# VectorE in place of accumulating DMAs for two chunks' down sums; S5 outputs one step later; the compression's small loads ahead

## The chip, the cores and the metric

One core of one Trainium2 chip runs the whole layer as one program. The metric is the device time in microseconds of one execution of that program. Its engines are TensorE (matmuls; PE in the profile, PEld for its weight loads), VectorE (DVE), ScalarE (ACT), GpSimd (POOL) and SyncE (SP, which here only issues DMAs).

## The reference, cut to what matters

One layer of a hybrid decoder on 256 tokens of width 2048, all in float32. The hidden width of both feed-forward halves is 5632.

```
def swiglu(x, w1, w3, w2):
    return (jax.nn.silu(x @ w1) * (x @ w3)) @ w2

h = h + 0.5 * swiglu(rmsnorm(h, ffn1_norm), ffn1_w1, ffn1_w3, ffn1_w2)
proj = rmsnorm(h, mix_norm) @ w_in
q, kc, vc, ksl, vsl, kw, vw, gates, u_ssm = jnp.split(proj, splits, axis=-1)
a = nsa_mixer(q, kc, vc, ksl, vsl, kw, vw, gates, ...)   # attention over compressed, selected and window keys
s = s5_mixer(u_ssm, ...)                                 # state space model, gelu, gated linear unit
h = h + jnp.concatenate([a, s], axis=-1) @ w_out
h = h + 0.5 * swiglu(rmsnorm(h, ffn2_norm), ffn2_w1, ffn2_w3, ffn2_w2)
out = rmsnorm(h, final_norm)
```

The attention compresses keys and values: each block of 32 positions plus a position table (`cmp_pe`) goes through a small two-layer network (`cmp_w1`, gelu, `cmp_w2`). The S5 mixer runs a scan over 64 complex states for each group of 16 channels, adds a skip term, and passes the result through gelu and a gated linear unit.

## The kernel before, in words

**Precision and weights.** A float32 product is made from three matmuls of halves: ScalarE makes the high half of a weight tile (`whi`), VectorE the low half (`wlo`), both in `split` (lines 138 and 139); TensorE multiplies high by high, high by low and low by high (lines 191 to 193). `wload` (line 163) has SyncE load 512 KB of weights, two tiles of 128 rows by 512 columns, into a buffer of the pool `raw`. `wtiles` feeds a loop of matmuls with such pairs.

**The feed-forward half-steps.** `ffn` goes through the hidden width in 11 chunks of 512. For a chunk it forms the gates (columns of `w1` and `w3`), then two of the four column blocks of the previous chunk's down product (`down(c - 1, prev, (0, 1))`), transposes the gates (line 435), and does the other two blocks (`down(c - 1, prev, (2, 3))`). The chunks of `wino` are special: there the gates of some tiles are formed with seven products in place of eight (`up_wino`). The first half-step has the special chunks 1 to 5, the second 1 to 10. `down` adds each 128 by 512 sum into the residual `h` in `add`: VectorE does so in one instruction (line 372), but for the special chunks ScalarE writes half the sum to a tile `d` of the pool `work` (line 369) and GpSimd issues a DMA that adds `d` into `h` (line 370).

**Pools and phases.** There are two layouts of the on-chip memory, `"ffn"` and `"mixer"`; `layout` closes the pools `w`, `work` and `raw` of one and opens those of the other in the same space (the mixer has 3 weight buffers of each half, 40 work and 5 raw buffers, and a pool of small tiles behind them). A tile of a new pool waits for the tiles of the old one that lay there. The pool `hidden` (8 buffers) stays through all phases. The first half-step changes to the mixer layout ahead of chunk 6, through `begin={6: go_on}`, and then runs the S5 preparation (`prepare`, line 691) beside the chunks 6 to 10; its first step loads seven small tensors into `work` (lines 476 to 484). The layout changes back ahead of the second half-step (line 1056).

**What sets the order.** The program is written in one order, and a planner of the framework fixes each engine's queue when the program is built: by priority (mostly the order of the program, with the weight splits 50 places ahead) among what it takes to be ready. Each engine then works through its queue in order. Side work is written as generators; `tick`, called after each weight tile pair, takes one step of each (`sides`), so their instructions stand between the matmuls.

**S5 and compression.** Two such generators run in the mixer. `s5_run` goes through eight tiles of 128 channels: `s5_tile` copies inputs to a padded tile (line 755), forms the input products (line 760), turns and scans the states (lines 763 to 772), turns them back into `xs5` (lines 774 to 780), and then forms the output with a group of small matmuls that read `xs5` (lines 783 and 787), the skip term (line 790), and for every second tile gelu and split into `hs`. `compress_all` starts when three of the four `hs` are there: `compress` loads the position table (line 817), transposes it (line 819), forms the blocks (line 828), loads `cmp_w1` and multiplies (lines 833 and 837), sums four partial results with a matmul (line 843) and applies gelu. Its second layer's weights are loaded on lines 855 and 856 and used on lines 858 and 867.

Of the kernel before, what the change touches and what calls it, by code (L numbers as in the profile page):

```python
# [72 lines left out]
def hymba_layer(tc, x, ffn1_norm, ffn1_w1, ffn1_w3, ffn1_w2, mix_norm, w_in,  # L73
# [4 lines left out]
    V, S, G, PE, SP = nc.vector, nc.scalar, nc.gpsimd, nc.tensor, nc.sync  # L78
    ctx = ExitStack()
    xp = ctx.enter_context(tc.tile_pool(name="xt", bufs=4))  # L80
    hp = ctx.enter_context(tc.tile_pool(name="hidden", bufs=8))
    cp = ctx.enter_context(tc.tile_pool(name="const", bufs=1))
    wp = sp = rp = mp = lay = None
    phase = ExitStack()
# [197 lines left out]
    def ffn(w1, w3, w2, xs, rstd, done, by_tokens=False, wino=range(0), begin={}):  # L282


        last = FF // 512 - 1

        def wpair(raw):
            hi, lo = (wp.tile([128, 2, 512], F32R, name=k, tag=k) for k in ("whi", "wlo"))
# [71 lines left out]
        def down(c, ht, ns):  # L360
            def hx(kt):
                a, b = ht[kt // 2 % 2]
                return a[:, kt % 2, :], b[:, kt % 2, :]

            def add(n, tt, p):
                o = h[:, tt, n * 512:(n + 1) * 512]
                if c in wino and c != last:
                    d = work([128, 512])
                    S.activation(d, p, AF.Copy, scale=0.5)  # L369
                    G.dma_start(o, d, accum_op=ALU.add)  # L370
                    return
                V.scalar_tensor_tensor(o, p, 0.5, o, op0=ALU.mult, op1=ALU.add)

            def tail(ns):

                for tt in range(NT):
                    t = slice(tt * 128, tt * 128 + 128)
                    for n in ns:
                        p = mm_tile()
                        for kt in range(4 * c, 4 * c + 4):  # L380
                            (xh, xl), (hi, lo) = hx(kt), ws[n, kt]
                            PE.matmul(p, xh[:, t], hi, start=kt == 4 * c, stop=False)
                            PE.matmul(p, xh[:, t], lo, start=False, stop=False)
                            PE.matmul(p, xl[:, t], hi, start=False, stop=kt == 4 * c + 3)
                        add(n, tt, p)
                        done(n, (tt,))

            ws = {}
            for n in ns:
                if by_tokens and c == last:  # L390
                    if n == 2:
                        tail((2, 3))
                    if n >= 2:
                        continue
                    for kb in (4 * c, 4 * c + 2):
                        raw = wload(w2[kb * 128:(kb + 2) * 128, n * 512 + 1024:n * 512 + 1536], 512)
                        hi, lo = wpair(raw)
                        for i in range(2):
                            ws[n + 2, kb + i] = hi[:, i, :], lo[:, i, :]
                for tt, p in enumerate(gemm_rows(hx, w2, n * 512, 512, 4 * c, 4 * c + 4)):  # L400
                    add(n, tt, p)
                if c == last:
                    done(n)
# [4 lines left out]
        for c in range(FF // 512 + 1):  # L408
            if c in begin:
                sides.append(begin[c]())  # L410
            if c == wino[0]:
                drain(comb)
            if c in wino:
                gates = up_wino(c)
            elif c < FF // 512:
                ps1 = gemm_rows(xs, w1, c * 512, 512)
                gates = []
                for tt in range(NT):
                    sl = work([128, 512])
                    S.activation(sl, ps1[tt], AF.Silu, scale=rstd[:, tt:tt + 1])  # L420
                    gates.append(sl)
                ps3 = gemm_rows(xs, w3, c * 512, 512)
                for tt in range(NT):
                    V.scalar_tensor_tensor(gates[tt], ps3[tt], rstd[:, tt:tt + 1], gates[tt],
                                           op0=ALU.mult, op1=ALU.mult)
            if prev is not None:
                down(c - 1, prev, (0, 1) if c < FF // 512 else (0, 1, 2, 3))
            if c < FF // 512:
                ht = []
                for kp in range(2):  # L430
                    ps = tp_tile().rearrange("p (k t) -> p k t", k=2)
                    for k in range(2):
                        for tt in range(NT):
                            f = (2 * kp + k) * 128
                            PE.transpose(ps[:, k, tt * 128:tt * 128 + 128], gates[tt][:, f:f + 128], ident)
                    hh, hl = (hp.tile([128, 2, T], F32R, name="hd", tag="hd") for _ in range(2))
                    split(hh, hl, ps)
                    ht.append((hh, hl))
                if prev is not None:
                    down(c - 1, prev, (2, 3))  # L440
                prev = ht
# [306 lines left out]
    def s5_tile(i):  # L748
# [29 lines left out]
        V.tensor_tensor(b, b, sn, ALU.mult)  # L778
        V.tensor_tensor(d, d, cs, ALU.mult)
        V.tensor_tensor(xs5[:, 1, :, 1:129], b, d, ALU.add)  # L780
        yield
        y = tp_tile()[:, :256].rearrange("p (r c) -> p r c", r=2)
        PE.matmul(y[:, 0, :], s5.k0[i // 4][:, i % 4, :], uv[:, 0, :], start=True, stop=False, skip_group_check=True)
        for r, m in ((0, s5.ca), (1, s5.c)):
# [12 lines left out]
            hs.append((hh, hl))  # L797

    def s5_run():
        for i in range(8):  # L800
            while len(ut) <= i // 2:
                yield
            yield from s5_tile(i)

    def gelu2(o, y, shape):

# [4 lines left out]
        V.scalar_tensor_tensor(o, t, 1.0, y, op0=ALU.add, op1=ALU.mult)  # L811


    def compress(kc, pe, w1, b1):

        pr = work([32, 128])
        SP.dma_start(pr, pe[0])
        ps = tp_tile()
        PE.transpose(ps[:, :32], pr, ident[:32, :32])
        pt = work([128, 32])  # L820
# [18 lines left out]
            yield  # L839
        hp = work([128, 128])  # L840
        V.tensor_copy(hp, hid)
        ps = tp_tile()
        PE.matmul(ps[:, :32], hp, cst[:, C_SEL:C_SEL + 32], start=True, stop=True)
        xh = work([128, 30])
# [2 lines left out]
        return xh  # L847

    def compress_all():
        while not kcv or len(hs) < 3:  # L850
            yield
        hk = yield from compress(kcv[0], cmp_pe_k, cmp_w1_k, par[:, P_B1:P_B1 + 1])
        hv = yield from compress(kcv[1], cmp_pe_v, cmp_w1_v, par[:, P_B1 + 1:P_B1 + 2])
        w2k, w2v = work([128, 128]), work([128, 128])
        SP.dma_start(w2k, cmp_w2_k[0])
        SP.dma_start(w2v, cmp_w2_v[0])
        ps = tp_tile()
        PE.matmul(ps[:, :30], w2k, hk, start=True, stop=True)
        G.memset(kcb, 0.0)
        V.tensor_scalar(kcb[:, :, 0:15], ps[:, :30].rearrange("p (g c) -> p g c", g=2), 0.5, None, ALU.mult)  # L860
        for g in range(2):
            yield
            hx = work([128, 8, 16])
            G.memset(hx, 0.0)
            V.tensor_scalar(hx[:, :, 0:15], hv[:, None, g * 15:g * 15 + 15].to_broadcast([128, 8, 15]), 0.5, None, ALU.mult)
            ps = tp_tile()
            PE.matmul(ps[:, :128], hx.rearrange("p a c -> p (a c)"), w2v, start=True, stop=True)
            m = [work([128, 4, 128]) for _ in range(2)]
            for b in range(8):
                V.tensor_scalar(m[b // 4][:, b % 4, :], ps[:, :128], cst[:, C_ROW + b:C_ROW + b + 1], None, ALU.mult)  # L870
            vcb.append(m)
# [258 lines left out]
```

## Time and profile before

| What | Value |
|---|---|
| Time, median of 3 runs | 1833.62 us (1832.59 to 1834.07) |
| The profiled execution | 1834.84 us, span of its instructions 1833.1 us |
| TensorE busy | 1788.7 us, 98% of the span |
| VectorE busy | 1518.7 us, 83% |
| ScalarE busy | 998.1 us, 54% |
| GpSimd busy | 112.8 us, 6% |
| Accumulating DMAs `h<-wk` | 112, 256 KB each, 5.9 us from issue to landing (median) |
| Mean granted clock of TensorE | 0.991 |

A busy share says how long an engine had an instruction in work, not what it waited for. The rows further down are therefore mostly of two kinds: timelines, in which a row gives the start, the duration, the line, the operation with output and inputs, and in brackets the idle time before it with what ended it; and waits, in which a row says which engine and line waited for which, with the total, the number of times and the longest. `x2` says that instructions of the same kind in a row are merged. Lines are those of the kernel before.

### The profile page before, as it was taken

How to read it: one execution, taken by the hardware profiler on the slowest of the kernel's cores; microseconds unless marked ns; L12 is line 12 of the kernel's file. 1: busy time of each engine (PE TensorE's matmuls, PEld its weight loads, DVE VectorE, ACT ScalarE, POOL GpSimd, SP SyncE). 2: the span in 40 equal slices, each digit the busy share in tenths (PEclk: the TensorE clock that was granted, in tenths of full speed). 3: DMA queues.
4: the chain of work that ended last, by engine and by line, in shares of the span. 5: the costliest groups of instructions: out<-in, count | busy, mean ns of one | idle time of the engine just before them, and what ended most of it. 6: DMA issues, size and time to landing. Idle time of an engine off the chain costs nothing.

```text
span 1833.1 us, 25026 instructions
## 1 busy us (share of the span) xinstructions
PE 1788.7 (98%) x9140; PEld 1489.4 (81%) x9140; DVE 1518.7 (83%) x2150; ACT 998.1 (54%) x1364; POOL 112.8 (6%) x145
## 2 busy tenths in 40 slices
PE   8999999969999999999999999999999999999997
PEld 6888888858888878899988777888888888888886
DVE  7999998846788887769887557999899998988994
ACT  7556656524433434544536745555666656666664
POOL 0001011100100000000000000000111011001103
PEclk9999999979999999999999999999999999999999
DMA  7557888676755666555574356556887788787884
GB/s 267 178 179 240 264 220 239 179 189 201 220 178 162 183 195 192 166 140 154 154 219 151 114 172 218 154 191 214 239 248 223 248 223 237 227 271 191 247 279 117
DMA packets 209424, 370.28 MB, mean 202 GB/s; under 512 B 22827, under 2 KB 32661, under 8 KB 209301
## 3 DMA queue, kind: packets, MB, share of 16 engines
q1 hardware_dynamic: 193172, 339.31, 58.3%
q0 software_dynamic: 16128, 29.37, 9.4%
q8 instruction: 72, 1.18, 0.3%
q14 instruction: 52, 0.42, 0.1%
HBM read 337.16 MB, written 2.11 MB: 185 GB/s over the span
## 4 chain that ended last, share of the span: by engine, by line
PE 50%; DVE 4%; issue 1%; ACT 0%; DMA 0%; ACTq 0%; SPq 0%; DVEq 0%
PE mm L193 7%; PE mm L192 7%; PE mm L191 7%; PE tp L303 3%; PE tp L305 3%; PE tp L306 3%; PE mm L306 2%; PE mm L303 2%; PE mm L305 2%; PE sd L306 2%; PE sd L305 2%; PE sd L303 2%; PE mm L203 1%; PE mm L202 1%; PE mm L204 1%; DVE wlo L139 1%
## 5 line engine op out<-in xcount | busy, mean ns | idle before, releaser
L138 ACT ACTIVATE whi<-raw 128x1024 fp32r<-128x1024 f32 x699 | 716.0, 1056 | 596.1 <-PE mm L193 225.9
L139 DVE SCALAR_TENSOR_TENSOR wlo<-raw,whi 128x1024 fp32r<-128x1024 f32 x699 | 835.8, 1222 | 211.1 <-ACT whi L138 210.0
L191 PE MATMUL mm<-whi,hd 128*128 128x512 f32 x688 | 270.0, 392 | 0.0
L192 PE MATMUL mm<-wlo,hd 128*128 128x512 f32 x688 | 268.3, 390 | 0.8 <-DVE wlo L139 0.8
L193 PE MATMUL mm<-whi,hd 128*128 128x512 f32 x688 | 268.3, 390 | 0.0
L191 PE MATMUL mm<-whi,xh 128*128 128x512 f32 x576 | 230.1, 401 | 18.0 <-ACT whi L138 18.0
L192 PE MATMUL mm<-wlo,xh 128*128 128x512 f32 x576 | 230.1, 399 | 1.6 <-DVE wlo L139 1.4
L193 PE MATMUL mm<-whi,xl 128*128 128x512 f32 x576 | 228.4, 397 | 0.0
L370 POOL DMA_DIRECT2D h<-wk x112 | 97.9, 972 | 1180.6 <-ACT wk L369 998.7
L192 PEld LDWEIGHTS mm<-wlo,hd 128*128 128x128 f32 x688 | 129.2, 188 | 27.5 <-DVE wlo L139 1.5
L191 PEld LDWEIGHTS mm<-whi,hd 128*128 128x128 f32 x688 | 129.2, 188 | 26.7 <-issue 0.6
L193 PEld LDWEIGHTS mm<-whi,hd 128*128 128x128 f32 x688 | 129.2, 188 | 26.7
L191 PEld LDWEIGHTS mm<-whi,xh 128*128 128x128 f32 x576 | 109.7, 191 | 42.1 <-ACT whi L138 19.6
L192 PEld LDWEIGHTS mm<-wlo,xh 128*128 128x128 f32 x576 | 110.1, 191 | 27.4 <-DVE wlo L139 5.0
L193 PEld LDWEIGHTS mm<-whi,xl 128*128 128x128 f32 x576 | 110.1, 191 | 22.5 <-DVE xl L139 0.4
L202 PE MATMUL mm<-xh,whi 128*128 128x256 f32 x384 | 111.8, 292 | 0.9 <-DVE wk L1008 0.9
L203 PE MATMUL mm<-xh,wlo 128*128 128x256 f32 x384 | 109.3, 285 | 1.1 <-DVE wlo L139 1.1
L204 PE MATMUL mm<-xl,whi 128*128 128x256 f32 x384 | 108.7, 283 | 0.0
L369 ACT ACTIVATE wk<-mm 128x512 f32<-128x512 f32 x112 | 65.6, 595 | 73.2 <-PE mm L193 69.7
L303 PE MATMUL sd<-whi,xh 128*128 128x512 f32 x255 | 99.2, 389 | 0.0
L303 PE MATMUL tp<-whi,xh 128*128 128x512 f32 x255 | 99.2, 389 | 0.0
L305 PE MATMUL tp<-wlo,xh 128*128 128x512 f32 x255 | 99.2, 389 | 0.0
(299 smaller groups left out, 2954.1 us busy)
## 6 DMA issues: line engine op xcount, KB each, us to landing
raw<-in_ffn_w_dram SPq DMA_DIRECT2D x528, 512.0 KB, 4.8
h<-wk POOLq DMA_DIRECT2D x112, 256.0 KB, 5.9
raw<-in_w_in_dram SPq DMA_DIRECT2D x48, 512.0 KB, 3.7
raw<-in_w_out_dram SPq DMA_DIRECT2D x32, 512.0 KB, 3.7
raw<-in_w_in_dram SPq DMA_DIRECT2D x8, 536.0 KB, 4.5
raw<-in_glu_w_dram SPq DMA_DIRECT2D x8, 512.0 KB, 3.7
h<-in_x_dram SPq DMA_DIRECT2D x4, 512.0 KB
raw<-in_cmp_w_k_dram SPq DMA_DIRECT2D x4, 512.0 KB, 4.2
```

The lines of the kernel that those rows point to most:

```text
L138: S.activation(hi, src, AF.Copy if isinstance(scale, float) else AF.Identity, scale=scale)
L139: V.scalar_tensor_tensor(lo, src, scale, hi.bitcast(F32), op0=ALU.mult, op1=ALU.subtract)
L191: PE.matmul(o, xh[:, t], hi[:, i, :n], start=kt == k0, stop=False)
L192: PE.matmul(o, xh[:, t], lo[:, i, :n], start=False, stop=False)
L193: PE.matmul(o, xl[:, t], hi[:, i, :n], start=False, stop=kt == k1 - 1)
L202: PE.matmul(o, wh, xh, start=kt == 0 and q % 2 == 0, stop=False, skip_group_check=True)
L203: PE.matmul(o, wl, xh, start=False, stop=False, skip_group_check=True)
L204: PE.matmul(o, wh, xl, start=False, stop=last, skip_group_check=True)
L303: PE.matmul(o, xh, wh, start=id(o) not in begun, stop=False)
L305: PE.matmul(o, xh, wl, start=False, stop=False)
L306: PE.matmul(o, xl, wh, start=False, stop=stop)
L370: G.dma_start(o, d, accum_op=ALU.add)
```

## The change

Three things are edited.

1. In `add`, the limit for the accumulating DMA is now `by_dma`. In the first half-step it is 4, so chunks 1 to 3 go by DMA as before and chunks 4 and 5 are added by VectorE like the ordinary chunks. In the second half-step it is 10, as before.
2. `s5_tile` ends with the states, and the output part is a generator of its own, `s5_out`. `s5_run` takes the first step of the next tile, then the output of the tile before it, then the rest of the tile.
3. `compress_all` loads the two position tables and the two second-layer weights at its first step, into four buffers of the pool `hidden` (renamed `hd`), rather than where they are used; and `compress` gives up its turn once more between the copy of the partial results and the matmul that sums them.

```diff
--- before.py
+++ after.py
@@ -78,7 +78,7 @@
     V, S, G, PE, SP = nc.vector, nc.scalar, nc.gpsimd, nc.tensor, nc.sync
     ctx = ExitStack()
     xp = ctx.enter_context(tc.tile_pool(name="xt", bufs=4))
-    hp = ctx.enter_context(tc.tile_pool(name="hidden", bufs=8))
+    hd = ctx.enter_context(tc.tile_pool(name="hidden", bufs=8))
     cp = ctx.enter_context(tc.tile_pool(name="const", bufs=1))
     wp = sp = rp = mp = lay = None
     phase = ExitStack()
@@ -283,6 +283,7 @@
 
 
         last = FF // 512 - 1
+        by_dma = last if last in wino else wino.stop - 2
 
         def wpair(raw):
             hi, lo = (wp.tile([128, 2, 512], F32R, name=k, tag=k) for k in ("whi", "wlo"))
@@ -364,7 +365,7 @@
 
             def add(n, tt, p):
                 o = h[:, tt, n * 512:(n + 1) * 512]
-                if c in wino and c != last:
+                if c in wino and c < by_dma:
                     d = work([128, 512])
                     S.activation(d, p, AF.Copy, scale=0.5)
                     G.dma_start(o, d, accum_op=ALU.add)
@@ -433,7 +434,7 @@
                         for tt in range(NT):
                             f = (2 * kp + k) * 128
                             PE.transpose(ps[:, k, tt * 128:tt * 128 + 128], gates[tt][:, f:f + 128], ident)
-                    hh, hl = (hp.tile([128, 2, T], F32R, name="hd", tag="hd") for _ in range(2))
+                    hh, hl = (hd.tile([128, 2, T], F32R, name="hd", tag="hd") for _ in range(2))
                     split(hh, hl, ps)
                     ht.append((hh, hl))
                 if prev is not None:
@@ -778,7 +779,10 @@
         V.tensor_tensor(b, b, sn, ALU.mult)
         V.tensor_tensor(d, d, cs, ALU.mult)
         V.tensor_tensor(xs5[:, 1, :, 1:129], b, d, ALU.add)
-        yield
+
+    def s5_out(i):
+
+        uv = ut[i // 2][:, i % 2, :].rearrange("p (c r) -> p r c", r=2)
         y = tp_tile()[:, :256].rearrange("p (r c) -> p r c", r=2)
         PE.matmul(y[:, 0, :], s5.k0[i // 4][:, i % 4, :], uv[:, 0, :], start=True, stop=False, skip_group_check=True)
         for r, m in ((0, s5.ca), (1, s5.c)):
@@ -797,10 +801,19 @@
             hs.append((hh, hl))
 
     def s5_run():
+        out = iter(())
         for i in range(8):
             while len(ut) <= i // 2:
-                yield
-            yield from s5_tile(i)
+                if next(out, out) is out:
+                    yield
+            tile = s5_tile(i)
+            next(tile)
+            yield from out
+            yield
+            yield from tile
+            out = s5_out(i)
+            yield
+        yield from out
 
     def gelu2(o, y, shape):
 
@@ -811,10 +824,8 @@
         V.scalar_tensor_tensor(o, t, 1.0, y, op0=ALU.add, op1=ALU.mult)
 
 
-    def compress(kc, pe, w1, b1):
-
-        pr = work([32, 128])
-        SP.dma_start(pr, pe[0])
+    def compress(kc, pr, w1, b1):
+
         ps = tp_tile()
         PE.transpose(ps[:, :32], pr, ident[:32, :32])
         pt = work([128, 32])
@@ -839,6 +850,7 @@
             yield
         hp = work([128, 128])
         V.tensor_copy(hp, hid)
+        yield
         ps = tp_tile()
         PE.matmul(ps[:, :32], hp, cst[:, C_SEL:C_SEL + 32], start=True, stop=True)
         xh = work([128, 30])
@@ -847,13 +859,13 @@
         return xh
 
     def compress_all():
+        pk, pv, w2k, w2v = (hd.tile([n, 128], F32, name="hd", tag="hd") for n in (32, 32, 128, 128))
+        for t, src in ((pk, cmp_pe_k), (pv, cmp_pe_v), (w2k, cmp_w2_k), (w2v, cmp_w2_v)):
+            SP.dma_start(t, src[0])
         while not kcv or len(hs) < 3:
             yield
-        hk = yield from compress(kcv[0], cmp_pe_k, cmp_w1_k, par[:, P_B1:P_B1 + 1])
-        hv = yield from compress(kcv[1], cmp_pe_v, cmp_w1_v, par[:, P_B1 + 1:P_B1 + 2])
-        w2k, w2v = work([128, 128]), work([128, 128])
-        SP.dma_start(w2k, cmp_w2_k[0])
-        SP.dma_start(w2v, cmp_w2_v[0])
+        hk = yield from compress(kcv[0], pk, cmp_w1_k, par[:, P_B1:P_B1 + 1])
+        hv = yield from compress(kcv[1], pv, cmp_w1_v, par[:, P_B1 + 1:P_B1 + 2])
         ps = tp_tile()
         PE.matmul(ps[:, :30], w2k, hk, start=True, stop=True)
         G.memset(kcb, 0.0)
```

## Rows read from the trace of the kernel before

**Rows 1.** The page, 40 equal slices: granted TensorE clock in tenths.

```profile
PEclk9999999979999999999999999999999999999999
```

**Rows 2.** Table of stretches: PE, PEld, DVE, ACT, POOL busy us (count), clock, DMA.

```profile
360.00:380.00 20.00, 15.31 (x72) 12.41 (x70) 1.29 (x2) 4.56 (x8) 6.93 (x14) 0.94 0.60 103
380.00:400.00 20.00, 9.76 (x21) 6.52 (x22) 11.25 (x45) 4.23 (x4) 0.18 (x2) 0.59 0.92 233
...
400.00:460.00 60.00, 60.00 (x270) 49.13 (x269) 42.41 (x103) 28.70 (x34) 4.35 (x6) 0.99 0.70 206
...
1125.00:1128.00 3.00, 3.00 (x8) 2.31 (x8) 3.00 (x5) 3.00 (x5) 0.00 (x0) 0.50 1.02 330
```

**Rows 3.** Timeline of TensorE, 374 to 402 us: start us, us, line, idle before.

```profile
374.69 0.39 PE L192 MATMUL mm<-wlo,hd 128*128 128x512 f32 x1
374.92 0.39 PE L193 MATMUL mm<-whi,hd 128*128 128x512 f32 x1
385.88 1.22 PE L191 MATMUL mm<-whi,xh 128*128 128x512 f32 x2 [10.57 <-ACT whi L138]
387.14 0.80 PE L192 MATMUL mm<-wlo,xh 128*128 128x512 f32 x1
...
395.82 1.22 PE L191 MATMUL mm<-whi,xh 128*128 128x512 f32 x2 [4.27 <-ACT whi L138]
...
401.45 0.40 PE L191 MATMUL mm<-whi,xh 128*128 128x512 f32 x1
```

**Rows 4.** Timeline of ScalarE, 384 to 396 us.

```profile
384.78 1.06 ACT L138 ACTIVATE whi<-raw 128x1024 fp32r<-128x1024 f32 x1 [8.83 <-DMA raw<-in_ffn_w_dram]
...
394.71 1.06 ACT L138 ACTIVATE whi<-raw 128x1024 fp32r<-128x1024 f32 x1 [8.88 <-DMA raw<-in_ffn_w_dram]
```

**Rows 5.** Waits of SyncE's queue, 350 to 400 us: total, times, longest.

```profile
SPq L163 <- DMA h<-wk: 37.2, 1, 37.2
```

**Rows 6.** Timeline of SyncE's queue, 375 to 396 us.

```profile
380.91 0.37 SPq L163 DMA_DIRECT2D raw<-in_ffn_w_dram  x1
381.33 0.46 SPq L476 DMA_DIRECT2D wk<-in_ssm_lam_re_dram  x1
...
389.08 3.46 SPq L163 DMA_DIRECT2D raw<-in_ffn_w_dram  x5
```

**Rows 7.** Instructions on tile h, VectorE's line: durations min, median, max.

```profile
L372 DVE SCALAR_TENSOR_TENSOR h<-mm,h x64: 679/685/774, 106.1 to 1823.2; 128x512 f32<-128x512 f32 x64
```

**Rows 8.** Timeline of TensorE, 362.5 to 366 us: the transposes of the gates.

```profile
363.35 1.04 PE L435 MATMUL tp<-cst,wk 128*128 128x128 f32 x8
```

**Rows 9.** Timeline of GpSimd, 358 to 362 us.

```profile
359.53 0.74 POOL L722 MEMSET ones<- 128x128 f32 x1
```

**Rows 10.** Timeline of VectorE, 1113 to 1120 us, second layout change.

```profile
1113.67 1.23 DVE L139 SCALAR_TENSOR_TENSOR wlo<-raw,whi 128x1024 fp32r<-128x1024 f32 x1 [2.57 <-ACT whi L138]
```

**Rows 11.** Timeline of SyncE's queue, 1112 to 1120 us.

```profile
1114.92 3.52 SPq L163 DMA_DIRECT2D raw<-in_ffn_w_dram  x7
```

**Rows 12.** Timeline of TensorE, 1119 to 1130 us, second layout change.

```profile
1123.51 0.73 PE L191 MATMUL mm<-whi,xh 128*128 128x512 f32 x2 [1.18 <-ACT whi L138]
...
1124.79 0.65 PE L192 MATMUL mm<-wlo,xh 128*128 128x512 f32 x1 [0.56 <-DVE wlo L139]
...
1128.54 0.39 PE L193 MATMUL mm<-whi,xl 128*128 128x512 f32 x1
```

**Rows 13.** Waits of TensorE, 790 to 975 us: total, times, longest.

```profile
PE tp L787 <- DVE xs L780: 1.3, 2, 0.7
...
PE tp L819 <- DMA wk<-in_cmp_pe_v_dram: 0.6, 1, 0.6
PE tp L787 <- DVE xs L776: 0.5, 1, 0.5
PE sd L760 <- ACT upad L755: 0.4, 1, 0.4
```

**Rows 14.** Line 755, the copies ahead of the input matmuls.

```profile
L755 ACT ACTIVATE upad<-wk x64: 297/316/336, 792.2 to 922.3; 32x128 f32<-32x128 f32 x64
```

## The prediction

> **What bounds the kernel now.** I read the slices of the page first: the only one in which TensorE's granted clock falls to 7 tenths is the ninth, 367 to 412 us [rows 1]. The table by stretches shows what that is: from 360 to 380 us TensorE is busy 15.31 of 20 us, from 380 to 400 us 9.76 of 20 at a mean clock of 0.59, and VectorE does 1.29 us of work in the first of the two [rows 2]. Elsewhere TensorE streams, as the stretch from 400 to 460 us does (60.00 of 60). So the place to look at is this hole, and not VectorE, busy as it is.
>
> TensorE's timeline gives its size. The last matmul of chunk 4's second down half starts at 374.92; the first of chunk 6 at 385.88 after 10.57 us of idling, a second hole of 4.27 us ends at 395.82, and full rate is back at 401.45 [rows 3]. Between 374.92 and 401.45 there are 24 matmuls, the 12 of each of two weight tiles. At the 0.23 us between starts before the hole (374.69 to 374.92) 25 steps take 5.75 us; they took 26.53. **The hole costs 20.8 us.**
>
> What ends it? TensorE waits for ScalarE's split of the raw weights (384.78, 394.71), and that for the load [rows 4]. SyncE's own waits say why the load is late: 37.2 us for one thing, the DMA that adds chunk 4's down sums into `h` [rows 5]. Its timeline: the first load of the new phase at 380.91, then seven small loads for the S5 preparation (381.33 onward), the second weight load only at 389.08 [rows 6]. So the chain is: last matmul, ScalarE's halving copy, GpSimd's issue, DMA landing shortly before 380.9, all of it because the copies `d` lie in the work pool of the old layout, over which the new pools are laid; then SyncE's issue, 4 us of load, the split. The second hole is the seven small loads' 7.75 us (381.33 to 389.08) on SyncE's queue ahead of load two.
>
> **The change, part by part.**
>
> *Down sums of chunks 4 and 5 on VectorE.* It removes 16 ScalarE copies, 16 GpSimd issues and 16 DMAs and adds 16 VectorE operations of 0.685 us, 11.0 us in all [rows 7]. Chunk 4's eight run between 358 and 377 us, where VectorE is nearly idle [rows 2]: nothing. Chunk 5's eight (5.5 us) follow from about 440 us on, in a stretch where VectorE has 17.6 of 60 us free [rows 2], but also TensorE's low halves to make on time; I take 0 and keep 5.5 for the range. If that cover were gone, TensorE would wait on `wlo`, as it does in later, fuller stretches.
>
> What matters is that nothing of chunk 4 is left in the old work pool after the transposes of chunk 5's gates, which end at 364.4 (363.35 plus 1.04) [rows 8]. Then the new raw pool should open some 16 us earlier. Two rows say that pools open one by one and not with the whole layout: the memsets in the mixer's small pool ran at 359.53, while chunk 4's down sums were still being multiplied [rows 9], and at the change back to the FFN layout SyncE issued seven raw loads in a row from 1114.92, the moment VectorE's last split of the old raw pool was done (1113.67 plus 1.23), while TensorE still worked [rows 10, 11]. So loads one to five (five raw buffers) go out near 364.4 and are there by 370. They also pass the seven small loads in SyncE's queue: these need the new work pool, over the old weight tiles, which TensorE reads to 375.3, and the planner orders by readiness (the memsets passed GpSimd work that the program has before them).
>
> **What is late next** is the new weight pool: it lies over the old weight tiles, so the first split waits for the last matmul's end, 374.92 plus 0.39 = 375.31. From the split's start to the first matmul is 1.10 us, and 2.36 us to the first that needs the low half (384.78 to 385.88 and 387.14) [rows 3, 4]. So it starts at 375.4, the third matmul at 377.76 instead of 375.61: 2.15 us remain. Then the clock: 380 to 400 us has a mean granted clock of 0.59 [rows 2]. At the second layout change the gaps are only 1.18 and 0.56 us, and still 1125 to 1128 us was granted 0.50, which is 1.2 GHz [rows 2]; 1124.79 to 1128.54 is 10 steps in 3.75 us instead of 2.3 [rows 12]. That is the nearest case, and I take its 1.5 us (0 to 1.7). The hole shrinks from 20.8 to 3.7 us (2.15 + 1.5): **17.1 us gained**, bounds 5.5 (rivals below) and 20.8 (no wait for the weight pool at all).
>
> The Trainium skill (TensorE: Matmul & The Clock Gate, Part 1) holds that only an idle gap of some length brings the clock down, and shorter ones leave it; by it the 1.5 us would not be paid and the total would be 1813.0. The rows of the second layout change speak against that, since gaps of 1.18 and 0.56 us are followed by half clock there.
>
> The seven small loads then occupy SyncE from 375.4 to 383.2, and load six can be split 5.6 us later (389.08 to 394.71 for the nearest one), at 388.8; TensorE has it at 389.9. Five tiles of 12 matmuls at 0.23 us last TensorE to 377.3 (two steps before 377.76) + 13.8 + 1.5 = 392.6. It fits with 2.7 us to spare, so the second hole goes too.
>
> *S5 outputs one step later.* The group of 17 small matmuls of an output now stands behind the next tile's first two input matmuls, and VectorE's skip-add behind two multiplications (2 x 0.68). No instruction is added, and a pair of tiles still takes eleven steps. TensorE's waits for the states are 1.3 and 0.5 us in 790 to 975 us [rows 13]; they should mostly go.
>
> *Small loads of the compression ahead, two steps more.* The loads move from the middle of the stage to SyncE's queue at its start, past weight loads that wait for free raw buffers there: four issues of about 0.5 us, hidden. TensorE's wait of 0.6 us for the position table goes [rows 13]. The two added steps delay attention by two ticks, which the GLU and output products cover. Parts two and three have 2.4 us of waits to win; reordering can also make new ones, at worst the longest of these, 0.7 us, at each of the eight outputs, 5.6 us. The old waits name their cause and the new ones would need one, so I take **2.0 us**, with 2.4 and minus 5.6 as ends.
>
> **Sum.** The profiled execution took 1834.84 us (span 1833.1 and 1.7 around it); 1834.8 - 17.1 - 2.0 = 1815.7. The median of the runs shown is 1833.62, 1.2 less, so the forecast is **1814.5 us**. The likeliest case's own range is 1810 to 1820.
>
> **Rivals.**
>
> (a) *The small loads keep their place ahead of load two.* Then load one is early, but SyncE stands at the first small load until 375.3 and load two goes out at 383.2 instead of 389.08. Only that 5.9 us is won: 1833.6 - 5.9 - 2.0 = 1825.7. For it: this is their order now [rows 6]. Against: now all become ready at one moment, and then they will not.
>
> (b) *The raw pool waits for the last matmul too.* Load one at 375.4 instead of 380.91 is 5.5 us: 1826. Against: the second layout change, where raw loads went out with TensorE still reading weights.
>
> (c) *The change does not open the pool*: another tile holds it as long. The hole stays and only the 2.0 us come: 1831.6, not told from no change. Against: SyncE's only long wait names the DMA [rows 5].
>
> (d) *Slower: TensorE meets the next tile's input before ScalarE has it.* Those input matmuls now stand ahead of the outputs, in order, and need eight ScalarE copies of 0.316 us (2.5 us) [rows 14], with a 1.06 us weight split possibly before them: 3.6 us on seven tiles, 25 us, so 1833.6 - 17.1 + 25 = 1841.5. It decides from 2.5 us per tile (7 x 2.5 = 17.5 against 17.1). Against: the same copies stood before the same matmuls so far and cost TensorE 0.4 us [rows 13].
>
> **How the numbers follow.** Forecast 0.74, (a) 0.09, (b) 0.07, (c) 0.05, (d) 0.05. A measurement of this kernel tells 0.2%, 3.7 us, from no change. Faster: forecast, (a) and (b), 0.90; within it: (c), 0.05; slower: (d), 0.05. The range goes from 1810 (20.8 and 2.4 us both won give 1810.4) to 1828, which takes in (a) and (b) with a part of the 5.5 us of VectorE or of the 5.6 us of new waits lost.
>
> **What would show it.** In the trace after: no wait of SyncE for the accumulating DMA near 375 us; five raw loads near 364, ahead of the seven small ones; TensorE's gap at the layout change under 2 us and no second one; chunk 6 some 17 us earlier against the transposes of chunk 5; no TensorE wait for the position table, little for the states. The prediction is wrong if raw loads still start after 375 us, if the small loads come before load two, if chunk 5's sums make `wlo` late, or if the stage from 780 to 975 us grows.

## The result, and the profile after

The changed kernel takes **1815.62 us** (median of 4 runs, 1813.4 to 1817.65), the kernel before on the same chip 1833.69 us (4 runs, 1832.59 to 1834.07). The ratio is 0.9902, with a 95% interval of 0.9885 to 0.9919: 18.1 us, or 1.0%, faster. The forecast was 1814.5 us, the range 1810 to 1828. The profiled execution took 1816.18 us, with a span of 1814.4 us and a mean granted clock of 0.996.

Line numbers have moved: 372 is 373 in the changed kernel, 435 is 436, 477 stands for 476, 727 is 728, 755 is 756, 787 is 791, and the compression's sums, 837 before, are line 848.

The page of the changed kernel: busy time by engine, the clock in 40 slices, and the accumulating DMAs that are left (96, where there were 112).

```profile
PE 1783.4 (98%) x9140; PEld 1488.5 (82%) x9140; DVE 1528.2 (84%) x2166; ACT 990.0 (55%) x1348; POOL 99.0 (5%) x129
...
PEclk9999999999999999999999999999999999999999
...
L371 POOL DMA_DIRECT2D h<-wk x96 | 84.0, 977 | 1044.3 <-ACT wk L370 862.8
```

The slice at 7 tenths [rows 1] is gone. The table of stretches of the changed kernel (busy us of PE, PEld, DVE, ACT, POOL with counts, then clock, DMA share, GB/s) answers to [rows 2]:

```profile
360.00:380.00 20.00, 18.33 (x85) 14.61 (x84) 9.90 (x13) 4.08 (x6) 1.83 (x9) 1.00 0.53 148
380.00:400.00 20.00, 20.00 (x90) 16.58 (x89) 17.36 (x60) 8.57 (x10) 0.00 (x0) 1.00 0.94 263
400.00:460.00 60.00, 58.79 (x267) 48.26 (x266) 47.61 (x125) 24.79 (x27) 0.78 (x3) 1.00 0.63 188
```

From 360 to 460 us TensorE idles 1.67 + 0 + 1.21 = 2.9 us, where it idled 14.9, and the clock stays full. Between the transposes of chunk 5's gates and those of chunk 6's it now takes 433.82 - 363.03 = 70.8 us; before it was 451.61 - 363.35 = 88.3. So **17.5 us of the 18 come from the layout change alone**. Timeline of TensorE, the start in chunk 6 before (chunk 5's is in [rows 8]), then both starts in the changed kernel:

```profile
451.61 1.03 PE L435 MATMUL tp<-cst,wk 128*128 128x128 f32 x8
```

```profile
363.03 1.03 PE L436 MATMUL tp<-cst,wk 128*128 128x128 f32 x8
...
433.82 1.03 PE L436 MATMUL tp<-cst,wk 128*128 128x128 f32 x8
```

Timeline of SyncE's queue in the changed kernel, 342 to 401 us (a row gives start and duration of a merged run of issues), which answers to [rows 6]:

```profile
342.27 24.31 SPq L163 DMA_DIRECT2D raw<-in_ffn_w_dram  x7
374.99 0.34 SPq L477 DMA_DIRECT2D wk<-in_ssm_lam_re_dram  x1
...
381.62 0.58 SPq L485 DMA_DIRECT2D wk<-in_ssm_c_im_dram  x1
382.30 18.03 SPq L163 DMA_DIRECT2D raw<-in_ffn_w_dram  x10
```

The merged first row holds the last two loads of the old layout (342.27 and 343.40) and five of the new one, the first at 364.10; it ends at 342.27 + 24.31 = 366.58. These five are the ones that used to go out at 380.91 and from 389.08 on. The seven small loads stand behind them, from 374.99. SyncE's waits from 340 to 400 us (total, times, longest) show the same: no DMA into `h` is among them any more [rows 5].

```profile
SPq L163 <- DVE wlo L139: 13.4, 5, 10.5
SPq L477 <- PE mm L193: 8.4, 1, 8.4
...
SPq L163 <- PE tp L436: 3.3, 1, 3.3
```

The second row is the small loads' wait for the last matmul on the old weight tiles, the third the new raw loads' wait for chunk 5's transposes. VectorE's timeline shows what took the place of the eight DMAs of chunk 4, the first of four such pairs up to 374.32 us:

```profile
357.11 1.37 DVE L373 SCALAR_TENSOR_TENSOR h<-mm,h 128x512 f32<-128x512 f32 x2 [0.48 <-PE mm L193]
```

TensorE's timeline over the change, which answers to [rows 3]:

```profile
374.57 0.39 PE L193 MATMUL mm<-whi,hd 128*128 128x512 f32 x1
376.11 0.73 PE L191 MATMUL mm<-whi,xh 128*128 128x512 f32 x2 [1.15 <-ACT whi L138]
377.37 0.50 PE L192 MATMUL mm<-wlo,xh 128*128 128x512 f32 x1 [0.53 <-DVE wlo L139]
377.70 0.40 PE L193 MATMUL mm<-whi,xl 128*128 128x512 f32 x1
...
405.39 0.24 PE L535 MATMUL tp<-cst,wk 32*128 32x32 f32 x1 [1.21 <-DVE wk L528]
```

Two gaps of 1.15 and 0.53 us are left of 10.57 and 4.27, full rate follows at once, and there is one new wait: the small transposes of the S5 preparation (line 535) for VectorE, 1.21 us.

Later, in the mixer's stage, something got worse. TensorE's waits from 780 to 975 us in the changed kernel, against [rows 13]:

```profile
PE sd L848 <- DMA raw<-in_cmp_w_v_dram: 2.6, 1, 2.6
...
PE tp L791 <- DVE xs L777: 0.5, 1, 0.5
...
PE tp L791 <- DVE xs L781: 0.2, 1, 0.2
```

The waits for the states fell from 1.8 to 0.7 us and the one for the position table is gone, but the value sums of the compression now wait 2.6 us for their own weights, which is more than the 1.7 us that these two gave.

### The profile page after: what moved, and what is told of

It is laid out like the page before. It is cut to its first block, busy times and chain, and to the rows that moved or that the text cites. A ratio compares the mean times of both kernels' runs of the same rounds, so it can differ in the third digit from the quotient of the medians.

```text
span 1814.4 us, 24981 instructions
## 1 busy us (share of the span) xinstructions
PE 1783.4 (98%) x9140; PEld 1488.5 (82%) x9140; DVE 1528.2 (84%) x2166; ACT 990.0 (55%) x1348; POOL 99.0 (5%) x129
## 3 DMA queue, kind: packets, MB, share of 16 engines
q8 instruction: 72, 1.18, 0.3%
## 4 chain that ended last, share of the span: by engine, by line
PE 52%; DVE 3%; issue 1%; DMA 1%; ACT 0%; ACTq 0%; DVEq 0%
PE mm L193 7%; PE mm L192 7%; PE mm L191 7%; PE tp L304 3%; PE tp L306 3%; PE tp L307 3%; PE mm L307 3%; PE mm L304 3%; PE mm L306 3%; PE sd L307 2%; PE sd L304 2%; PE sd L306 2%; PE mm L202 2%; PE mm L203 2%; PE mm L204 2%; DVE wlo L139 1%
## 5 line engine op out<-in xcount | busy, mean ns | idle before, releaser
L371 POOL DMA_DIRECT2D h<-wk x96 | 84.0, 977 | 1044.3 <-ACT wk L370 862.8
L307 PE MATMUL sd<-whi,xl 128*128 128x512 f32 x255 | 99.2, 389 | 0.0
```

The source lines that it names most:

```text
L307: PE.matmul(o, xl, wh, start=False, stop=stop)
```

## The experiments

Theory: the gain is the early opening of the raw pool at the first layout change, by the down sums alone, and the queue order that comes with it; parts two and three together give nothing, because one of their pieces makes the new wait. The rivals: parts two and three have a share of the gain; both chunks' sums are needed; early loads alone do it, whatever SyncE issues next.

### One part alone: e1 and e2

e1, against the kernel before:

```
+        by_dma = last if last in wino else wino.stop - 2
...
-                if c in wino and c != last:
+                if c in wino and c < by_dma:
```

> Only part one: VectorE adds the down sums of chunks 4 and 5; S5 and compression as before. Theory: this part carries the whole gain, 17 to 18 us by TensorE's timeline up to chunk 6 (the transposes of chunk 6's gates come 17.5 us earlier in the changed kernel), so about 1816.2 us. Rival: the VectorE additions cost some 2 us later on and parts two and three win them back: then about 1818.

e2, against the changed kernel:

```
-                if c in wino and c < by_dma:
+                if c in wino and c != last:
```

> Only parts two and three: S5 outputs a step later, small loads ahead, the added steps; chunks 4 and 5 by accumulating DMA as before. Theory: no measurable change, 1833.7 within 1 us, because the 2.4 us of waits that go are replaced by TensorE's new wait of 2.6 us for the last load of the compression's value weights and slower matmuls behind it; the 20.8 us hole at the layout change is unchanged. Rival, as predicted: 2.0 us faster, about 1831.7.

Measured: e1 1816.91 us (ratio 0.9909, 0.9893 to 0.9924). e2 1833.35 us (0.9997, 0.9988 to 1.0005): no change. The longest of TensorE's waits in e2 are the old hole and the new wait for the value weights:

```profile
PE mm L191 <- ACT whi L138: 18.5, 4, 10.5
...
PE sd L848 <- DMA raw<-in_cmp_w_v_dram: 2.2, 1, 2.2
```

So the down sums carry the whole gain, and the other two parts give nothing when taken together: the forecast's 2.0 us for them is refuted as a net figure.

### One of the two chunks: e5

Chunk 4's sums by VectorE, chunk 5's still by DMA (the other parts undone):

```
-                if c in wino and c != last:
+                if c in wino and (c < by_dma or by_dma < c < last):
```

> Part one for chunk 4 alone: VectorE adds its down sums, chunk 5 goes by accumulating DMA as before; S5 and compression as before. Theory: only the copies that lie in the old work pool at the layout change matter, and chunk 5's already lie in the new one, so the hole is closed as with both chunks: 1816 to 1817 us, TensorE's waits at the change 1.1 and 0.5 us. Rival: chunk 5's DMAs cost something of their own in the following 80 us: 1818 or more.

Measured: 1816.26 us (0.9901, 0.9886 to 0.9916), and the waits from 360 to 460 us are those of the changed kernel:

```profile
PE mm L191 <- ACT whi L138: 1.1, 1, 1.1
PE tp L535 <- DVE wk L528: 1.0, 1, 1.0
PE mm L192 <- DVE wlo L139: 0.5, 1, 0.5
```

Chunk 4's eight copies alone held the pool. Chunk 5's eight additions are neither needed nor a burden: with them (e1) and without them the time is the same within the runs. One thing differs from the changed kernel: half clock follows the two gaps in e5's trace, some 1.5 us (last section).

### The queue order: e8

The changed kernel, with the four weight loads after the first held behind the last of the seven small loads:

```
+        follow = behind and len(held) < 4
+        with tc.issue_after(behind[0]) if follow else nullcontext():
+            SP.dma_start(raw[:, :kq, :n], src.rearrange("(k p) n -> p k n", p=128))
...
-        SP.dma_start(cn[1], c_im[0].rearrange("(i g) h p -> (g h) i p", g=8))
+        behind.append(SP.dma_start(cn[1], c_im[0].rearrange("(i g) h p -> (g h) i p", g=8)).ins)
```

> The changed kernel with the next four weight loads after the first one of the mixer layout held behind the seven small loads in SyncE's queue, as they stood before. Theory: the order in that queue is worth the second hole: SyncE stands at the first small load to 375.0, load two goes out near 382.3, can be split 5.6 us later at 387.9, and TensorE, done with tile one at 380, has it at 389.0; 9 us of hole and 1.7 us of slow matmuls, about 1826 us. Rival: the small loads' DMAs take little and load two lands in 4 us with a shorter queue: 3 to 5 us slower than the changed kernel, about 1820.

Measured: 1824.79 us (0.9949, 0.9934 to 0.9963), 9.2 us over the changed kernel. SyncE's queue, and TensorE's longest wait:

```profile
364.11 0.37 SPq L165 DMA_DIRECT2D raw<-in_ffn_w_dram  x1
375.01 0.34 SPq L482 DMA_DIRECT2D wk<-in_ssm_lam_re_dram  x1
...
382.11 9.60 SPq L165 DMA_DIRECT2D raw<-in_ffn_w_dram  x6
```

```profile
PE mm L196 <- ACT whi L138: 14.5, 4, 10.2
```

This is rival (a), built as an experiment: it gives half of the gain back. It was priced at 1825.7, 0.9 us off. That the planner put five weight loads ahead of the small ones is worth 9 us by the medians, and the prediction gave this rival the highest chance of the four (0.09). At the layout change itself the price is higher: from chunk 5's transposes to chunk 6's e8 takes 445.01 - 363.05 = 82.0 us, 11.2 more than the changed kernel. Part of that comes back in the mixer's stage, where its wait for the value weights is 1.6 us and not 2.6 and the clock stays full behind it.

### Where parts two and three lost their gain: e3, e4, e7, e11

e3 undoes part three (the small loads of the compression, and its added step); e4 undoes part two; e7 takes only the added step out (one line, which runs once for the keys and once for the values, so it is the prediction's two added steps); e11 keeps it and gives the last eight blocks of value weights a place of their own.

```
e3     def compress(kc, pe, w1, b1):
+        pr = work([32, 128])
+        SP.dma_start(pr, pe[0])
...
e7         V.tensor_copy(hp, hid)
-        yield
         ps = tp_tile()
...
e11 +        early = [hd.tile([128, 512], F32, name="hd", tag="hd") for _ in range(2)]
+        for q, t in enumerate(early):
+            SP.dma_start(t.rearrange("p (l n) -> p l n", n=128),
+                         cmp_w1_v[0][(24 + 4 * q) * 128:(28 + 4 * q) * 128, :].rearrange("(l p) n -> p l n", p=128))
```

> Parts one and two, the compression as before (its small loads where they are used, no added step). Theory: TensorE's wait of 2.6 us for the value weights is gone, the wait of 0.6 us for the position table is back, the waits for the states stay low: about 1814, 1 to 2 us faster than the changed kernel. Rival: the reordered S5 outputs make that wait, and it is still there: about 1816.

> Parts one and three, S5 as before. Theory: TensorE's wait of about 2.6 us for the value weights is there, and its waits for the states (1.8 us) are back: 1816 to 1818. Rival: the wait for the value weights comes from the S5 order and is gone: about 1815.

> The changed kernel without the added step in the compression (the small loads stay ahead). Theory: the added step lets the raw buffers fill with value weights that wait for their blocks, and so makes TensorE's wait of 2.6 us; without it neither that wait nor the one for the position table is there: about 1812.5 us, 3 us faster than the changed kernel. Rival: the loads moved ahead make it, since the blocks and with them the weight loads are placed otherwise: the wait is still there, about 1815.6.

> The changed kernel, with its added step of the compression kept, and the last eight blocks of the compression's value weights loaded early into two buffers of another kind that are free then. Theory: with the added step the raw buffers are full of value weights, and the last load goes out too late; with a place of its own it is there in time, the wait of 2.6 us of the value sums goes and with it the lower clock behind it: 1812.5 to 1813.5 us. Rival: the step itself costs, whatever the buffers do (another load or the blocks of the next weight wait in its place): it stays at 1815 to 1816 us.

Measured: e3 1813.25 us (0.9888, 0.9874 to 0.9901), e4 1815.93 (0.9903, 0.989 to 0.9917), e7 1812.56 (0.988, 0.9865 to 0.9895), e11 1812.36 (0.9881, 0.9865 to 0.9898). The wait for the value weights is there in e4 (2.1 us) and in e2, and absent from e3, e7 and e11. TensorE's longest waits from 780 to 975 us, e7 and then e11:

```profile
PE mm L202 <- DVE wk L1019: 0.6, 1, 0.6
PE tp L791 <- DVE xs L777: 0.5, 1, 0.5
```

```profile
PE mm L202 <- DVE wk L1026: 0.6, 1, 0.6
...
PE sd L850 <- DMA raw<-in_cmp_w_k_dram: 0.5, 1, 0.5
```

How the added step makes the wait is to be seen in the changed kernel. TensorE's timeline, then SyncE's queue and its wait from 900 to 935 us, then the table of two stretches:

```profile
925.27 1.61 PE L848 MATMUL sd<-raw,wk 128*32 128x128 f32 x48 [0.18 <-issue]
...
931.94 0.64 PE L848 MATMUL sd<-raw,wk 128*32 128x128 f32 x16 [2.60 <-DMA raw<-in_cmp_w_v_dram]
```

```profile
925.96 0.37 SPq L844 DMA_DIRECT2D raw<-in_cmp_w_v_dram  x1
```

```profile
SPq L844 <- PE sd L848: 6.9, 2, 6.2
```

```profile
932.00:936.00 4.00, 4.00 (x36) 3.80 (x37) 3.21 (x5) 1.06 (x1) 0.00 (x0) 0.68 0.87 270
936.00:940.00 4.00, 4.00 (x32) 4.00 (x32) 2.83 (x5) 1.06 (x1) 0.00 (x0) 0.89 0.72 264
```

The weights of the key and value sums and those of the input product go through the same five raw buffers. The step puts the value sums a tick later (925.27, in e7 921.92), while three of their four loads are out by 914.93, so the buffers fill with value weights that nothing uses yet. The last load can go out only when a value block has been used: SyncE waits 6.2 us for the sums and issues it at 925.96 (in e7 at 919.75, ahead of the sums), and the input product's next weights stand behind it. TensorE runs 48 of the 64 sums and what it has of the input product, waits 2.60 us, and the clock is down for 8 us behind that: 4 x 0.32 + 4 x 0.11 = 1.7 us more by the granted clock of the two stretches. Together 4.3 us.

The whole stage, from the first matmul on line 728 (it spreads the norm's factors) to the first transpose on line 252 behind the output product, bears that out. The kernel before, the changed kernel, then e7:

```profile
774.72 0.68 PE L727 MATMUL tp<-wk,ones 128*128 128x128 f32 x4 [0.47 <-PE mm L204]
...
1085.27 0.44 PE L252 MATMUL tp<-cst,h 128*128 128x128 f32 x2
```

```profile
756.91 0.68 PE L728 MATMUL tp<-wk,ones 128*128 128x128 f32 x4 [0.47 <-PE mm L204]
...
1067.77 0.44 PE L252 MATMUL tp<-cst,h 128*128 128x128 f32 x2
```

```profile
757.55 0.68 PE L728 MATMUL tp<-wk,ones 128*128 128x128 f32 x4 [0.47 <-PE mm L204]
...
1064.30 0.44 PE L252 MATMUL tp<-cst,h 128*128 128x128 f32 x2
```

That is 310.6 us in the kernel before, 310.9 in the changed kernel and 306.8 in e7. So without the added step parts two and three do win 3.8 us, and in the changed kernel the step takes all of it back. Counted the same way, e1 takes 310.8 us and e3 308.6: the S5 order alone wins 2.2 of the 3.8 us, the small loads ahead 1.8. e11 shows by another way that the buffers make the wait: the step stays, the wait goes. Its stage takes 308.4 us, so 1.6 us more than e7's, which no run takes apart. e8 too keeps the step, has a shorter wait with the clock full behind it, and takes 308.2 us: the step's whole 4.1 us includes a drop of the clock that does not come each time. The kernels e7 and e11 are 3 us ahead of the changed kernel by their medians. That is 0.17%, less than one pair of measurements can tell for sure; the trace's 4.1 us of the stage is the better evidence. Both are about 21 us faster than the kernel before.

### What is left of the hole: e9, e10, e12, e13

In the changed kernel TensorE still waits 1.15 + 0.53 us for the first split, which waits for the old weight tiles under the new weight pool, and 1.21 us on line 535. e9 (on top of e3) and e10 (on top of e7) put the pools down in another order, so that the new weights lie where the old layout is free earlier. e12 is e10 with 32 unused bytes more in the mixer's small pool, e13 is e7 with 32 unused bytes ahead of the mixer's pools.

```
e9  +        order = ("work", "raw", "w") if name == "ffn" else ("w", "raw", "work")
e10 +        order = ("raw", "work", "w") if name == "ffn" else ("raw", "small", "w", "work")
+        at = {k: phase.enter_context(tc.tile_pool(name=k + "_" + name, bufs=lay.get(k, 1))) for k in order}
+        wp, sp, rp, mp = at["w"], at["work"], at["raw"], at.get("small")
...
e12 +            mp.tile([128, 8], F32, name="gap", tag="gap")
...
e13 +            phase.enter_context(tc.tile_pool(name="gap", bufs=1)).tile([128, 8], F32, name="gap")
```

> Parts one and two with the compression as before, and the pools laid in another order: work, raw, weights in the feed-forward layout and weights, raw, work in the mixer's, so that the new weight pool lies over the old work pool and not over weight tiles that TensorE still reads. Theory: what is left of the hole is the wait for the old weight pool, so TensorE's waits of 1.1 and 0.5 us at the first layout change go: 2 us faster than parts one and two alone (1813.25), about 1811; if the second layout change is held by the same thing, its 1.2 and 0.6 us and the slow matmuls behind them go too: 1808. Rival: the split is late for another reason (ScalarE's order): no change, 1813.

> The changed kernel without its added step of the compression, and with the buffer pools put down in another order, so that the raw weight buffers that open a layout lie where the layout before it is done earliest, for both kinds of layout. Theory: what TensorE still waits for at the first layout change (1.1 + 0.5 us, and part of the 1.2 us of the preparation's transposes behind it) is place in the work buffers, and goes; at the second layout change the raw loads are not held by ScalarE's last squares this time: 1809 to 1811 us, against 1812.56 of the kernel without the added step. Rival: the second layout change is held by another pool in turn, or the first change is bound by the weight splits: 1812 to 1814 us.

> The kernel with the other pool order and without the added step (e10), with one unused tile of 8 numbers per partition more in the mixer's small pool, so that the weight tiles and work buffers behind it begin 32 bytes further on, at a multiple of 64 bytes; in e10 they began 32 bytes past one, and there alone TensorE's step between starts in the mixer's layout was 0.234 us instead of 0.227 us. Theory: the address is what slowed the step: the step is 0.227 us again, the 6 us that e10 lost behind the first layout change come back, and with its closed hole the total is 1810 to 1811.5 us. Rival: the step is slowed by what lies beside the weights in the order of the pools, or by this run of the chip: it stays at 0.234 us and the total at 1817 us.

> The kernel without the added step (e7, pools in their usual order), with an unused tile of 32 bytes per partition put ahead of the mixer's pools, so that its weight tiles, work and raw buffers all begin 32 bytes past a multiple of 64. Theory of the address: TensorE's step in the mixer's layout goes from 0.227 to 0.234 us, about 6 us on 934 counted steps from 460 to 750 us and the others of the layout: 1818 to 1821 us against 1812.56. Rival (order of the pools, not the address): 0.227 us and 1812 to 1813 us.

Measured: e9 1814.2 us (0.9893, 0.9877 to 0.991), e10 1817.04 (0.9907, 0.9892 to 0.9921), e12 1812.74 (0.9883, 0.9866 to 0.9899), e13 1818.45 (0.9915, 0.99 to 0.993).

The waits at the first layout change are indeed gone: TensorE waits for nothing from 362 to 420 us in e10 and e12, and for 0.7 us in e9. But each reordering lost these 2 to 3 us, or more, elsewhere. In e9 it is the second layout change, where the FFN's raw pool now lies over the mixer's work pool. TensorE's wait there, then ScalarE's last instruction on that pool; the eleven loads behind it start at 1098.45:

```profile
PE mm L193 <- ACT whi L140: 4.9, 1, 4.9
```

```profile
1098.20 0.18 ACT L226 ACTIVATION_READ_ACCUMULATOR wk<-h 128x1 f32 x1
```

So the pool that gives one change its early loads takes them from the other one. e10's order has no such loss (1.2 + 0.6 us at the second change, as in the changed kernel), and yet it was 4.5 us slower than e7, which neither its theory nor its rival had. Its 512-column matmuls in the mixer's layout are slower. A group of TensorE's instructions from 440 to 750 us (busy us, mean ns of one), e7 and then e13 (e10 has 399 ns, e12 398):

```profile
L191 PE MATMUL mm<-whi,xh 128*128 128x512 f32 x256 | 100.5, 393 | 0.0
```

```profile
L193 PE MATMUL mm<-whi,xh 128*128 128x512 f32 x256 | 101.8, 398 | 0.0
```

Counted from start to start in the timeline, the median step is 0.227 us in e7 and 0.234, 0.233 and 0.234 us in e10, e12 and e13, with the full clock granted in each. In the feed-forward layout of the same four traces, where the weight tiles lie at a multiple of 128 bytes, it is 0.227 us, so it is not the chip on which a kernel ran. e13 differs from e7 by nothing but the addresses of the mixer's pools, and pays 5.9 us: the address is the cause, and the order of the pools is not. The theory for e12, that a multiple of 64 bytes is enough, fell: its step stayed at 0.233 us. In all kernels with 0.227 us the mixer's weight tiles begin at a multiple of 128 bytes of their partition (byte 84096 in the programs of e7 and e9); they begin 32 bytes past one in e10 and e13 and 64 past one in e12. In e9 the work buffers begin 64 bytes past one and the step is 0.227 us, and e10's raw buffers begin as in e7, at multiples of 64 bytes. These matmuls read the weight tiles and neither of the others, so it is most likely the weights' address that counts; no run moved the weights alone. That 128 is the number is only what agrees with all of these; no run set out to test it. The price is alike in the three: from chunk 6's transposes to line 728's first matmul e10, e12 and e13 take 329.2, 328.4 and 328.3 us and e7 323.1. Why e12 is still 4.3 us faster than e10 isn't settled: 1.1 us of it are in by 761 us, and 2.8 us come in the stage behind, where the matmuls of 256 columns step by 121.5 ns in the mean in e12 and by 123.9 in e10.

## Why the prediction was right

**The bound.** Right. The hole was the only place: 17.5 us gained between two points of TensorE's timeline, 17.1 forecast.

**What holds the raw pool.** Right, and e5 narrows it: chunk 4's eight copies alone. The raw loads went out between the transposes of chunk 5 (363.03 + 1.03 = 364.06) and 366.58, as forecast (364.4), with TensorE on the old weights until 375. That is against rival (b), and against (c).

**Order of the queue.** Right: the small loads moved behind. e8 shows the price had it been otherwise.

**What is late next.** The weight pool, as named: the third matmul starts at 377.37 instead of 374.57 + 3 x 0.23 = 375.26. That is 2.1 us, 2.15 forecast.

**The clock behind the gaps.** The 1.5 us at half clock was not paid in the execution that was profiled. In the changed kernel 378 to 381 us ran at full clock:

```profile
378.00:381.00 3.00, 3.00 (x15) 2.48 (x14) 1.58 (x2) 1.04 (x1) 0.00 (x0) 1.00 1.09 108
```

Here the rule of the Trainium skill (TensorE: Matmul & The Clock Gate, Part 1), that only an idle gap of some length brings the clock down, came out; the last section shows that it is not the whole of it. In e5 the same two gaps were followed by half clock, so neither outcome could be forecast from them, and that the term was not paid here is luck. In the place of the 1.5 us came 1.2 us that the forecast did not have, the preparation's transposes waiting on VectorE (line 535): VectorE has 17.36 us of work from 380 to 400 us where it had 11.25 [rows 2]. That the hole had been its slack too fits this, and no run tests it. So the sum of the boundary was 20.8 - 2.1 - 1.2 = 17.5 and not 20.8 - 3.7: right in size by two errors that cancel.

**The second hole.** Gone, as forecast: TensorE is busy for 20.00 us of 380 to 400.

**VectorE's sixteen additions.** Nothing, as taken. In the stretch from 400 to 460 us VectorE went from 42.41 [rows 2] to 47.61 us of work, and no matmul there waits for a low half.

**Parts two and three.** Wrong, and this is the term that was mis-sized: "I take **2.0 us**". Net it was nothing: 310.6 us for the stage before, 310.9 after, and e2 at a ratio of 0.9997. Most of the waits that the forecast named did go, and by e7 they and what follows from them were worth 3.8 us. By the same trace the stage did not shrink, which was close to one of the forecast's own signs of being wrong, a stage that grows. What failed is the sentence that the two added steps are covered. It weighed attention, which the steps delay, and not the raw buffers, which are held longer while the step passes: TensorE's new wait of 2.6 us and the 1.7 us of lower clock behind it took back the 3.8. The forecast had asked for a named cause of any new wait; the cause was in the code, five buffers shared by two products, and only the lower bound of minus 5.6 us held a place for it.

**Rival (d).** TensorE's wait for the copies of line 756 is 0.4 us, as before [rows 13]. Its mechanism did not appear.

The total missed by 1.1 us of 1815.6: 2.0 us too many for parts two and three, 0.4 too few at the boundary, and the rest lies within what the runs differ by. So the main mechanism was right, and a miss this small is partly luck.

## What to carry to other kernels

When buffers are laid over one another between phases, ask which instruction touches the old pool last, and not which one is busiest: here eight accumulating DMAs, issued by an engine that is 6% busy, held the weights of the next phase for nearly 17 us (364.10 against 380.91), and moving their sums to the busiest helper engine cost no time that a run shows. Before adding a step between producer and consumer, list the buffers that stay occupied during it and what is loaded through them next. A reordering of pools moves both ends of each lifetime, and it also moves addresses, so the step of an untouched inner loop is to be read again after it.

## What the runs showed of the hardware that was not expected

**The address of the weight tiles.** 32 bytes of shift lengthened the median step of the 512-column matmuls of a layout from 0.227 to 0.234 us, 3%, at full clock and without a wait (e13 against e7).

**The clock after the same gaps.** Gaps of 1.15 and 0.53 us at the first layout change left the clock full in the changed kernel (1.00 above), but not in e5, where the same two gaps were followed by half clock (0.52, mostly the level of 1.2 GHz). At the second layout change, gaps of 1.18 and 0.55 us were followed by half clock in the changed kernel, as before [rows 2], and gaps of 1.19 and 0.55 us by full clock in e12. Stretches of e5, of the changed kernel and of e12:

```profile
378.00:381.00 3.00, 3.00 (x9) 2.33 (x8) 1.68 (x2) 0.04 (x1) 0.00 (x0) 0.52 1.08 107
```

```profile
1108.00:1111.00 3.00, 3.00 (x8) 2.31 (x7) 3.00 (x7) 3.00 (x5) 0.00 (x0) 0.51 0.98 319
```

```profile
1106.00:1109.00 3.00, 3.00 (x15) 2.48 (x14) 3.00 (x7) 3.00 (x5) 0.00 (x0) 1.00 0.96 279
```

So the length of the gap does not decide alone, and the rows of one place do not give the clock at another: such a term of about 1.5 us belongs in the range and not in the sum.
